# Loads of h tiles by their places, splits moved between engines, rotary tables in two tiles, stores on ScalarE's queue

## The chip, the cores and the metric

The kernel runs on one core of one Trainium2 chip. The metric is device time in microseconds of one execution; for the kernel before it is the median of three runs. The engines are TensorE (PE, matmul and transposes), VectorE (DVE), ScalarE (ACT), GpSimd (POOL) and SyncE (SP), which here only issues DMAs.

## The reference

One layer of an encoder trunk, applied to two groups of 1024 tokens ("prompt" and "sample") with the same weights, in float32:

```python
for each group:                                   # x is (1, 1024, 1024)
    qa, ka, va, qb, kb, vb = split(x @ w_in)      # 2304 columns
    oa = rms_norm(dilated windows, three patterns, joined by their denominators) (rope(qa), rope(ka), va)
    ob = rms_norm(grouped attention(axial_rope(rms_norm(qb)), axial_rope(rms_norm(kb)), vb))
    x = layer_norm(alpha * x + concat(oa, ob) @ w_o)
    x = layer_norm(alpha * x + cross_attention(x, mem))        # 4 heads, 256 memory tokens
    gate, val = split(x @ w_up)                                # 2 x 2816 columns
    h = gelu(depthwise_conv3(gate) + conv_b) * val
    x = layer_norm(alpha * x + h @ w_down)
```

## The kernel before

The two groups run one after the other, each through phase_in (input projection, rotary, stores of q, k, v), attention, phase_mid (output projection, cross attention), ffn_up and ffn_down; between the first group's phase_in and attention stands cross_prep for both. A float32 product is made of three matmuls of rounded operands: every operand is split into a high half (a rounded copy) and a low half (the operand minus the high half), and mm3 (lines 125 to 129) issues high x high, high x low, low x high. So every operand that reaches TensorE costs two instructions elsewhere. split (lines 113 to 115) puts the high half on ScalarE (line 109) and the low half on VectorE (line 115). wsplit (lines 117 to 123) puts both on GpSimd (lines 122 and 123), with act=True the high half on ScalarE and with dve=True the low half on VectorE.

The order of the work on each engine is set by the framework's planner, which runs a simulation of the program in the order in which it is written; it puts an instruction ahead of earlier ones when they are not ready, and each engine then keeps that order. DMAs are issued by SP, in the order of its own list, so that one which waits holds up those behind it.

phase_in: x arrives in eight tiles of 128 tokens through two buffers (xl); x_in (line 295) loads one and splits it, in group 0 tiles 1 and 3 by wsplit and the others by split. Weights come in chunks of 512 columns through three raw buffers (raw, line 82, shared by all phases) and six split tiles (wts). In chunk 0 the first four token tiles are accumulated together, the others follow. The rotary tables (tabs, 128 x 8 x 8 x 64) are one tile; load_tabs (line 310) loads it in group 0 in four DMAs, multiplies half of it by the two norm gains on GpSimd (lines 322 and 327) and stores it to DRAM (tabd), from which group 1 loads it in one DMA (line 312). rope (line 331) multiplies on VectorE (lines 337 and 343) and adds on GpSimd (line 345).

phase_mid and ffn_up: the up projection works on sums and differences of quarters of x and w_up with seven products instead of eight (numbers 1 to 7). x2t (line 900) transposes one tile of normalized x (line 903), evacuates it (lines 908 and 911), and after each second tile forms sums (lines 882 to 888) and splits blocks of them (block, line 867); late (line 894) splits further quarters with pool=True, by wsplit. standardize (line 798) normalizes a tile: statistics on VectorE, a power on GpSimd (line 140), the product on ScalarE (line 807). In ffn_up the first column block, f = 0, is done in two half products: all seven products on the first half of the tokens, with the last x2t after product 5, then all seven on the second half. Its weights are split with the high half on ScalarE and the low half on VectorE for all seven (the dve argument); later blocks use VectorE for 6, 7, 5 and 3.

ffn_down: the 22 tiles of h (128 x 1024) and w_down are multiplied in four passes: tiles 0 to 11 for output columns 0 to 511, tiles 0 to 11 for columns 512 to 1023, tiles 12 to 21 for columns 0 to 511, and the same for the rest. One step takes one h tile against eight token tiles, 24 matmuls of 512 columns. h_in (line 1135) loads an h tile into a raw buffer and splits it into one of 14 slots; tiles 14 to 21 take the slots of tiles 0, 1, 2, 7, 8, 9, 10 and 11. wd_in (line 1144) loads and splits w_down for two steps, through the same raw buffers. In the second pass h_in is called once in each step until all 22 are loaded. In the fourth pass each output tile is normalized by layernorm (lines 780 to 795, with the power at 140) and stored (line 1213).

Of the kernel before, what the change touches and what calls it, by code (L numbers as in the profile page):

```python
# [18 lines left out]
NT = 8  # L19
# [52 lines left out]
class Trunk:  # L72
# [43 lines left out]

    def wsplit(self, hi, lo, raw, act=False, dve=False):
        nc = self.nc
        if act:
            self.copy(hi, raw)  # L120
        else:
            nc.gpsimd.tensor_scalar(hi, raw, 1.0, 0.0, op0=ALU.mult, op1=ALU.add)  # L122
        return (nc.vector if dve else nc.gpsimd).tensor_sub(lo, raw, hi.bitcast(F32))  # L123
# [14 lines left out]
    def rpow(self, out, ms, _=None):  # L138

        self.nc.gpsimd.tensor_tensor(out, ms, self.neghalf[:, :1].to_broadcast(list(ms.shape)), op=ALU.pow)  # L140
# [144 lines left out]
    def phase_in(self, g, S, tabd):  # L285
# [6 lines left out]
        xl, tabp, wk, vs, t1p = P("xl", 2, "left"), P("tabs"), P("rope", 2), P("vs", 3), P("t1p", 4)  # L292
        xT = []

        def x_in(ct):
            xt = xl.tile([128, 8, 128], F32, name="xt")
            t8 = self.t8.tile([128, 2, 8, 128], F32R, name="t8")
            n = 2 if g == 0 and ct == 0 else 1
            for j in range(n):
                k = slice(j * 8 // n, (j + 1) * 8 // n)  # L300
                nc.sync.dma_start(xt[:, k], xd[ct, :, k])
                if g == 0 and ct in (1, 3):
                    self.wsplit(t8[:, 0, k], t8[:, 1, k], xt[:, k])
                else:
                    self.split(t8[:, 0, k], t8[:, 1, k], xt[:, k])
            xT.append(t8)

        tabs = tabp.tile([128, NT, 8, 64], F32, name="tabs")

        def load_tabs():  # L310
            if g:
                nc.sync.dma_start(tabs, tabd)
                return

            with self.tc.issue_after(self.w_dma.ins):
                for j in range(0, NT, 2):
                    nc.sync.dma_start(tabs[:, j:j + 2], a["tabs"][:, j:j + 2])
            for q, gn in ((0, "q_norm_g"), (1, "k_norm_g")):
                gt = tabp.tile([128, 64], F32, name=f"gt{q}")
                nc.sync.dma_start(gt, bcast_rows(a[gn], 64))  # L320
                c, s = tabs[:, :, 4 + 2 * q], tabs[:, :, 5 + 2 * q]
                nc.gpsimd.tensor_mul(c, c, gt[:, None, :].to_broadcast([128, NT, 64]))
                sv = s.rearrange("p t (a b e) -> p t a b e", a=2, b=2)
                gv = gt.rearrange("p (a b e) -> p a b e", a=2, b=2)
                for aa in range(2):
                    for b in range(2):
                        nc.gpsimd.tensor_mul(sv[:, :, aa, b], sv[:, :, aa, b],
                                             gv[:, None, aa, 1 - b].to_broadcast([128, NT, 16]))
            nc.sync.dma_start(tabd, tabs)

        def rope(p, nh, ct, tab, half):
# [4 lines left out]
            c, s = tabs[:, ct, tab], tabs[:, ct, tab + 1]  # L336
# [50 lines left out]
        for ch in range(5):  # L387
            if ch == 1 and g == 0:
                self.conv_constants()
            if ch == 4 and g == 0:  # L390
                self.mem_in(xl)
# [418 lines left out]
    def phase_mid(self, g, S, o2s, ob, G, U, yD):  # L810
# [56 lines left out]
        def block(i, j, src, pool=False):  # L867

            c = slice(j * 128, j * 128 + 128)
            (self.wsplit if pool else self.split)(bt[i][0][:, :, c], bt[i][1][:, :, c], src.rearrange("p (k t) -> p k t", k=4))  # L870
# [162 lines left out]
    def ffn_up(self, B, todo, hD):  # L1033
# [74 lines left out]
        ready = [weights(0, (6, 1, 7, 5, 2, 4, 3))]  # L1108
        for f in range(NFF):
            e = begin(f)  # L1110
            if f == 0:

                for i in ORDER:
                    prod(e, i, 0)
                    if i == 5:
                        x2t()
# [38 lines left out]
    def ffn_down(self, B, yD, hD, out):  # L1155
# [23 lines left out]
        for lo, hi, n in ((0, K0, 0), (0, K0, 1), (K0, NFF, 0)):  # L1179
# [6 lines left out]
            for f in range(lo, hi):  # L1186
# [10 lines left out]
                elif len(hs) < NFF:  # L1197
# [9 lines left out]
        for ct in range(NT):  # L1207
# [5 lines left out]
            nc.sync.dma_start(out[ct * 128:(ct + 1) * 128], yt(ct))  # L1213
# [89 lines left out]
```

## Time and profile before

| | |
|---|---|
| median of the runs | 3304.3 us (3292.97, 3304.3, 3304.65) |
| profiled execution | 3311.24 us, span 3309.4 us |
| granted TensorE clock, mean of the span | 0.981 |
| TensorE matmul | 3190.4 us busy, 96% of the span |
| TensorE weight load | 2712.0 us, 82% |
| VectorE | 1772.7 us, 54% |
| GpSimd | 1559.3 us, 47% |
| ScalarE | 1210.5 us, 37% |

Times within the profile are microseconds from the start of the span. A busy TensorE is not TensorE at its peak, so its idle stretches and its granted clock are read beside its busy time. A wait in the profile has the engine's instruction, and behind an arrow the instruction that it waited for; a window is a stretch of the span with the busy time and the count of instructions of each engine in it. Group 0 fills the first half of the span, group 1 begins at about 1747.

### The profile page before, as it was taken

Reading aid. Unit: us, or ns where it says so; the run is one execution under the profiler, and the core shown is the slowest. Engines: PE = TensorE matmul, PEld = TensorE weight load, DVE = VectorE, ACT = ScalarE, POOL = GpSimd, SP = SyncE. Lnnn points to the kernel's source line nnn. Section 1 sums busy time; section 2 is a strip of 40 time slices with the busy share of each in tenths; the row PEclk is TensorE's granted clock in tenths of the full one; section 3 lists DMA queues with packets and bytes.
Section 4 is the critical chain, followed back from the end, with each engine's and each line's share of the span. In section 5 each row is a group of like instructions: output and inputs, shape, how many; then the busy total and the mean of one; then the engine's idle time right before and its main releaser. Section 6 shows DMA issues by size and latency. Waiting matters only on the chain.

```text
span 3309.4 us, 42941 instructions
## 1 busy us (share of the span) xinstructions
PE 3190.4 (96%) x16425; PEld 2712.0 (82%) x16425; DVE 1772.7 (54%) x2975; ACT 1210.5 (37%) x2355; POOL 1559.3 (47%) x1173
## 2 busy tenths in 40 slices
PE   7999999999999999999898999999999999999988
PEld 6888899888887888888687889888888788888867
DVE  5242156884536766556135255688444676665414
ACT  2122156882333434331002126688143443333101
POOL 4473500774435655543336450277343665554242
PEclk9999999999999999999899999999999999999999
DMA  6455486003121222235225368500211132224421
GB/s 230 129 169 187 167 213 173 14 7 99 42 77 51 78 88 83 89 129 177 92 71 190 118 164 185 142 14 23 90 51 64 58 96 77 83 77 170 141 89 51
DMA packets 292578, 351.63 MB, mean 106 GB/s; under 512 B 17980, under 2 KB 211732, under 8 KB 291476
## 3 DMA queue, kind: packets, MB, share of 16 engines
q1 hardware_dynamic: 292084, 348.82, 34.3%
q8 instruction: 129, 2.11, 0.3%
q14 instruction: 77, 0.63, 0.1%
q10 hardware_dynamic: 288, 0.07, 0.0%
HBM read 252.24 MB, written 100.79 MB: 107 GB/s over the span
## 4 chain that ended last, share of the span: by engine, by line
PE 89%; DMA 3%; DVE 2%; POOL 2%; ACT 1%; issue 1%; SPq 1%; POOLq 0%; ACTq 0%; DVEq 0%
PE pS L1069 11%; PE pT L1069 7%; PE pO L1069 7%; PE pO L127 7%; PE pO L129 7%; PE pO L128 7%; PE pT L127 7%; PE pT L129 7%; PE pT L128 7%; PE pO L697 4%; PE pT L686 3%; PE pS L670 3%; PE pO L593 2%; PE pS L554 2%; PE pS L127 2%; PE pS L128 2%
## 5 line engine op out<-in xcount | busy, mean ns | idle before, releaser
L123 POOL TENSOR_TENSOR wts<-raw,wts 128x512 fp32r<-128x512 f32 (+1 forms) x229 | 470.8, 2062 | 220.0 <-ACT wts L109 215.4
L1069 PE MATMUL pS<-t,wts 128*128 128x512 f32 (+1 forms) x1656 | 378.7, 382 | 1.1 <-DVE t L115 1.0
L1069 PEld LDWEIGHTS pS<-t,wts 128*128 128x128 f32 x1656 | 304.4, 190 | 60.5 <-DVE t L115 1.2
L127 PE MATMUL pT<-wts,t 128*128 128x512 f32 (+1 forms) x864 | 340.0, 394 | 8.7 <-ACT wts L109 8.3
L129 PE MATMUL pT<-wts,t 128*128 128x512 f32 (+1 forms) x864 | 335.9, 389 | 11.2 <-DVE t L115 11.2
L128 PE MATMUL pT<-wts,t 128*128 128x512 f32 (+1 forms) x864 | 336.0, 389 | 0.5 <-DVE wts L123 0.5
L127 PE MATMUL pO<-wts,t 128*128 128x512 f32 (+1 forms) x816 | 322.1, 395 | 5.4 <-DVE t L343 3.8
L128 PE MATMUL pO<-wts,t 128*128 128x512 f32 (+1 forms) x816 | 317.2, 389 | 4.2 <-POOL wts L123 4.2
L129 PE MATMUL pO<-wts,t 128*128 128x512 f32 (+1 forms) x816 | 316.6, 389 | 0.3 <-DVE t L115 0.3
L122 POOL TENSOR_SCALAR wts<-raw 128x1024 fp32r<-128x1024 f32 (+1 forms) x88 | 102.2, 1165 | 380.0 <-DMA raw<-w_down 242.3
L1069 PE MATMUL pT<-t,wts 128*128 128x512 f32 (+1 forms) x1104 | 258.0, 382 | 1.4 <-ACT t L109 1.0
L1069 PE MATMUL pO<-t,wts 128*128 128x512 f32 (+1 forms) x1104 | 256.9, 380 | 0.5 <-ACT res L109 0.4
L122 POOL TENSOR_SCALAR ptb<-praw 128x512 fp32r<-128x512 f32 x116 | 72.8, 628 | 382.0 <-ACT praw L109 230.9
L1069 PEld LDWEIGHTS pT<-t,wts 128*128 128x128 f32 x1104 | 203.2, 190 | 41.2 <-ACT t L109 1.2
L1069 PEld LDWEIGHTS pO<-t,wts 128*128 128x128 f32 x1104 | 202.0, 189 | 40.1 <-ACT res L109 0.5
L129 PEld LDWEIGHTS pT<-wts,t 128*128 128x128 f32 x864 | 163.6, 189 | 44.2 <-DVE t L115 11.7
L127 PEld LDWEIGHTS pT<-wts,t 128*128 128x128 f32 x864 | 164.4, 190 | 40.1 <-ACT wts L109 8.3
L128 PEld LDWEIGHTS pT<-wts,t 128*128 128x128 f32 x864 | 163.9, 190 | 32.7 <-DVE wts L123 1.0
L127 PEld LDWEIGHTS pO<-wts,t 128*128 128x128 f32 x816 | 155.9, 191 | 37.2 <-issue 4.2
L128 PEld LDWEIGHTS pO<-wts,t 128*128 128x128 f32 x816 | 154.8, 190 | 34.3 <-POOL wts L123 4.5
L129 PEld LDWEIGHTS pO<-wts,t 128*128 128x128 f32 x816 | 154.6, 189 | 31.9 <-DVE t L115 0.8
L673 DVE TENSOR_REDUCE mn<-pS 128x1 f32<-128x1024 f32 x128 | 155.9, 1218 | 42.1 <-PE pS L670 41.0
(272 smaller groups left out, 6804.7 us busy)
## 6 DMA issues: line engine op xcount, KB each, us to landing
raw<-w_up SPq DMA_DIRECT2D x88, 512.0 KB, 4.4
hD<-d SPq DMA_DIRECT2D x44, 512.0 KB, 5.2
raw<-hD SPq DMA_DIRECT2D x44, 512.0 KB, 4.5
raw<-w_down SPq DMA_DIRECT2D x44, 512.0 KB, 3.9
raw<-w_in SPq DMA_DIRECT2D x32, 512.0 KB, 4.5
kst<-ka SPq DMA_DIRECT2D x32, 512.0 KB, 10.3
qa<-vs SPq DMA_DIRECT2D x16, 512.0 KB, 3.9
ka<-vs SPq DMA_DIRECT2D x16, 512.0 KB, 3.6
```

The source lines that it names most:

```text
L122: nc.gpsimd.tensor_scalar(hi, raw, 1.0, 0.0, op0=ALU.mult, op1=ALU.add)
L123: return (nc.vector if dve else nc.gpsimd).tensor_sub(lo, raw, hi.bitcast(F32))
L127: mm(out, sh, mh, start=start, stop=False)
L128: mm(out, sh, ml, start=False, stop=False)
L129: mm(out, sl, mh, start=False, stop=stop)
L554: nc.tensor.matmul(o, qq, kk[hl], start=hl == 0, stop=hl == 1)
L593: nc.tensor.matmul(po[:, n * 64:(n + 1) * 64], pt[:, n, j], v, start=j == 0, stop=j == 1)
L670: nc.tensor.matmul(p[:, ns], q[:, ct * 128:(ct + 1) * 128], ks[:, hl, ns], start=hl == 0, stop=hl == 1)
L673: nc.vector.tensor_reduce(mn, p, axis=X, op=ALU.min)
L686: nc.tensor.transpose(p[:, c * 128:(c + 1) * 128], s[:, k * 128:(k + 1) * 128], self.ident)
L697: nc.tensor.matmul(po[:, :256], bd["v"][:, k, h // 4], hl[l][:, k].rearrange("p a b -> p (a b)"), start=k == 0 and l == 0, stop=k == 7 and ...
L1069: nc.tensor.matmul(p, w[:, x, k], b[l][:, k, cs], start=i in (1, 6, 7, 5) and k + x + l == 0, stop=k == 3 and x == 1, skip_group_check=True)
```

## The change

- x_in: in group 0, tiles 4 to 7 are split by the new hsplit (high half on ScalarE, low half on GpSimd) instead of split.
- block with pool=True, called by late, uses hsplit instead of wsplit: the high half goes from GpSimd to ScalarE.
- The rotary tables are two tiles of four token tiles each, in two pools, loaded and stored separately. The multiplication by the gains is a function of its own, called in group 0 before chunk 2 instead of right after the load, in twenty instructions instead of ten.
- ffn_up: for f = 0 the low halves of weights 2, 4 and 3 go to GpSimd, and the last x2t is written after all seven first half products instead of after product 5.
- ffn_down: in the second pass h_in is called in steps 0 to 4 and 8 to 11 only, and h tile 21 is left to the third pass, which loads it at its own step.
- The output stores are issued by ScalarE instead of SP.
- rpow loses an argument that was not used.

```diff
+    def hsplit(self, hi, lo, src):
+        self.wsplit(hi, lo, src, True)
...
-        xl, tabp, wk, vs, t1p = P("xl", 2, "left"), P("tabs"), P("rope", 2), P("vs", 3), P("t1p", 4)
+        xl, tabp, wk, vs, t1p = P("xl", 2, "left"), [P("tab0"), P("tab1")], P("rope", 2), P("vs", 3), P("t1p", 4)
...
                     self.wsplit(t8[:, 0, k], t8[:, 1, k], xt[:, k])
+                elif g == 0 and ct > 3:
+                    self.hsplit(t8[:, 0, k], t8[:, 1, k], xt[:, k])
...
-        tabs = tabp.tile([128, NT, 8, 64], F32, name="tabs")
+        tabs = [tabp[i].tile([128, 4, 8, 64], F32, name="tabs") for i in range(2)]
...
+            for i in range(2):
+                if g:
+                    nc.sync.dma_start(tabs[i], tabd[:, 4 * i:4 * i + 4])
+                    continue
+
+                with self.tc.issue_after(self.w_dma.ins):
+                    for j in range(0, 4, 2):
+                        nc.sync.dma_start(tabs[i][:, j:j + 2], a["tabs"][:, 4 * i + j:4 * i + j + 2])
+
+        def gain_tabs():
             for q, gn in ((0, "q_norm_g"), (1, "k_norm_g")):
...
+            for i in range(2):
+                nc.sync.dma_start(tabd[:, 4 * i:4 * i + 4], tabs[i])
...
+            if ch == 2 and g == 0:
+                gain_tabs()
...
-            (self.wsplit if pool else self.split)(bt[i][0][:, :, c], bt[i][1][:, :, c], src.rearrange("p (k t) -> p k t", k=4))
+            (self.hsplit if pool else self.split)(bt[i][0][:, :, c], bt[i][1][:, :, c], src.rearrange("p (k t) -> p k t", k=4))
...
-        ready = [weights(0, (6, 1, 7, 5, 2, 4, 3))]
+        ready = [weights(0, (6, 1, 7, 5))]
...
                 for i in ORDER:
                     prod(e, i, 0)
-                    if i == 5:
-                        x2t()
+                x2t()
...
-                elif len(hs) < NFF:
+                elif len(hs) < NFF - 1 and len(hs) - 12 <= f - (3 if f > 4 else 0) and not 4 < f < 8:
+
                     self.h_in(hD)
...
-            nc.sync.dma_start(out[ct * 128:(ct + 1) * 128], yt(ct))
+            nc.scalar.dma_start(out[ct * 128:(ct + 1) * 128], yt(ct))
```

## Rows read from the trace of the kernel before

**Rows 1.** TensorE's waits, longest first: instruction, releaser, us in total, times, longest.
```profile
PE pS L127 <- POOL wts L122: 29.8, 4, 7.5
PE pS L903 <- ACT res L807: 11.8, 2, 6.1
```
**Rows 2.** Windows of 50 us: PE, PEld, DVE, ACT, POOL busy (count), clock, DMA, GB/s.
```profile
1500.00:1550.00 50.00, 50.00 (x222) 41.42 (x221) 34.94 (x28) 6.55 (x7) 19.04 (x8) 1.00 0.64 220
1550.00:1600.00 50.00, 45.53 (x201) 37.35 (x199) 8.53 (x9) 4.24 (x4) 7.76 (x4) 0.99 0.24 80
1600.00:1650.00 50.00, 39.59 (x150) 31.83 (x151) 12.63 (x12) 4.24 (x4) 20.17 (x12) 0.81 0.29 97
...
3150.00:3200.00 50.00, 35.10 (x136) 28.17 (x136) 13.39 (x13) 5.30 (x5) 17.82 (x10) 0.86 0.27 90
```
**Rows 3.** Windows at the start of group 0, columns as above.
```profile
28.40:42.00 13.60, 1.41 (x6) 0.75 (x5) 13.59 (x4) 0.28 (x1) 12.39 (x9) 0.64 0.37 154
42.00:46.00 4.00, 4.00 (x10) 3.15 (x11) 0.54 (x2) 0.00 (x0) 1.27 (x1) 0.51 0.71 262
```
**Rows 4.** Second pass of ffn_down in time: start, us, instruction, [idle before, releaser].
```profile
1571.41 2.60 SPq L1138 DMA_DIRECT2D raw<-hD  x2
...
1595.56 1.06 ACT L109 ACTIVATE t<-raw 128x1024 fp32r<-128x1024 f32 x1 [26.14 <-PE pO L129]
...
1597.90 0.38 SPq L1147 DMA_DIRECT2D raw<-w_down  x1
...
1603.01 0.80 PE L127 MATMUL pS<-wts,t 128*128 128x512 f32 x1 [7.48 <-POOL wts L122]
```
**Rows 5.** Instructions on tile xt until 70 us: ns least, median, most; starts.
```profile
L115 DVE TENSOR_TENSOR t<-xt,t x7: 692/1224/12685, 4.5 to 61.6; 128x1024 fp32r<-128x1024 f32 x5, 128x512 fp32r<-128x512 f32 x2
```
**Rows 6.** Start of group 0 in time, GpSimd and TensorE.
```profile
28.38 1.06 POOL L122 TENSOR_SCALAR t<-xt 128x1024 fp32r<-128x1024 f32 x1
...
33.84 2.36 POOL L123 TENSOR_TENSOR t<-xt,t 128x1024 fp32r<-128x1024 f32 x1
...
41.93 0.80 PE L129 MATMUL pT<-wts,t 128*128 128x512 f32 x1 [11.24 <-DVE t L115]
```
**Rows 7.** Instructions on tile tabs until 80 us, GpSimd's: ns least, median, most.
```profile
L327 POOL TENSOR_TENSOR tabs<-tabs,gt x8: 461/467/482, 23.8 to 27.9; 128x128 f32<-128x128 f32 x8
...
L322 POOL TENSOR_TENSOR tabs<-tabs,gt x2: 1293/1293/1293, 22.5 to 25.4; 128x512 f32<-128x512 f32 x2
```
**Rows 8.** A window in which chunks 2 and 3 are projected, columns as above.
```profile
150.00:200.00 50.00, 50.00 (x230) 41.45 (x229) 15.69 (x41) 6.95 (x12) 30.28 (x23) 1.00 0.39 121
```
**Rows 9.** Windows at the start of the up projection, group 0.
```profile
1060.00:1066.00 6.00, 0.42 (x2) 0.42 (x3) 5.45 (x9) 4.28 (x7) 6.00 (x6) 0.76 0.31 88
1066.00:1088.00 22.00, 20.47 (x120) 18.99 (x119) 16.07 (x25) 8.66 (x17) 14.32 (x9) 0.83 0.14 49
```
**Rows 10.** Start of the up projection in time, group 0.
```profile
1053.23 3.48 DVE L123 TENSOR_TENSOR wts<-raw,wts 128x512 fp32r<-128x512 f32 x2
...
1065.58 1.97 PE L903 MATMUL pS<-ident,res 128*128 128x128 f32 x8 [5.79 <-ACT res L807]
...
1070.38 1.50 ACT L911 ACTIVATE res<-pS,ln2c 128x128 f32<-128x128 f32 x4
```
**Rows 11.** From group 0 to group 1 in time.
```profile
1746.13 1.99 ACT L109 ACTIVATE t<-xt 128x1024 fp32r<-128x1024 f32 x2
...
1766.91 0.46 SPq L1213 DMA_DIRECT2D out<-res  x1
...
1767.42 0.42 SPq L312 DMA_DIRECT2D tabs<-tabd  x1
...
1778.78 0.69 DVE L337 TENSOR_TENSOR t<-pO,tabs 128x512 f32<-128x512 f32 x1 [6.46 <-DMA tabs<-tabd]
...
1780.28 0.76 PE L127 MATMUL pO<-wts,t 128*128 128x512 f32 x1 [3.76 <-DVE t L343]
```
**Rows 12.** Window behind the wait for the tables, columns as above.
```profile
1776.00:1785.00 9.00, 5.24 (x18) 3.92 (x17) 6.22 (x13) 2.12 (x2) 2.96 (x3) 0.81 0.55 222
```

More of the change, by code (lines that the diff above doesn't have):

```diff
@@ L136, in dma, with rpow @@
             self.sp_last = self.nc.sync.dma_start(out, in_)
-    def rpow(self, out, ms, _=None):
+    def rpow(self, out, ms):
         self.nc.gpsimd.tensor_tensor(out, ms, self.neghalf[:, :1].to_broadcast(list(ms.shape)), op=ALU.pow)
@@ L306, in x_in @@
             xT.append(t8)
-        tabs = tabp.tile([128, NT, 8, 64], F32, name="tabs")
+        tabs = [tabp[i].tile([128, 4, 8, 64], F32, name="tabs") for i in range(2)]
         def load_tabs():
[L311 to L317, printed above, removed]
+            for i in range(2):
[6 more added lines that the diff above has]
+        def gain_tabs():
             for q, gn in ((0, "q_norm_g"), (1, "k_norm_g")):
-                gt = tabp.tile([128, 64], F32, name=f"gt{q}")
+                gt = tabp[1].tile([128, 64], F32, name=f"gt{q}")
                 nc.sync.dma_start(gt, bcast_rows(a[gn], 64))
-                c, s = tabs[:, :, 4 + 2 * q], tabs[:, :, 5 + 2 * q]
-                nc.gpsimd.tensor_mul(c, c, gt[:, None, :].to_broadcast([128, NT, 64]))
-                sv = s.rearrange("p t (a b e) -> p t a b e", a=2, b=2)
                 gv = gt.rearrange("p (a b e) -> p a b e", a=2, b=2)
[L325 to L329, printed above, removed]
+                for t in tabs:
+                    c, s = t[:, :, 4 + 2 * q], t[:, :, 5 + 2 * q]
+                    nc.gpsimd.tensor_mul(c, c, gt[:, None, :].to_broadcast([128, 4, 64]))
+                    sv = s.rearrange("p t (a b e) -> p t a b e", a=2, b=2)
+                    for aa in range(2):
+                        for b in range(2):
+                            nc.gpsimd.tensor_mul(sv[:, :, aa, b], sv[:, :, aa, b],
+                                                 gv[:, None, aa, 1 - b].to_broadcast([128, 4, 16]))
+            for i in range(2):
+                nc.sync.dma_start(tabd[:, 4 * i:4 * i + 4], tabs[i])
         def rope(p, nh, ct, tab, half):
@@ L335, in rope @@
             t2 = wk.tile([128, 512], F32, name="t2")[:, :nh * 64]
-            c, s = tabs[:, ct, tab], tabs[:, ct, tab + 1]
+            c, s = [tabs[ct // 4][:, ct % 4, i] for i in (tab, tab + 1)]
             nc.vector.tensor_mul(t1.rearrange("p (h e) -> p h e", h=nh), p.rearrange("p (h e) -> p h e", h=nh),
```

## The prediction

> **What bounds the kernel now.** The page gives the first answer: TensorE is busy nearly all the span, so only its holes and the stretches in which its clock is halved can be won. I therefore read the waits of TensorE first, longest total on top [rows 1]: four waits of 7.5 us for GpSimd's weight splits in the down projection, and two of about 6 us for ScalarE's standardizing at the start of the up projection. The second view cuts the span into stretches of 50 us and counts matmuls. A full stretch of 512-column matmuls has 222, that is 50 / 222 = 0.2252 us each; 1550 to 1600 has 201, 1600 to 1650 has 150, and in the second group 3150 to 3200 has 136 [rows 2]. Counting what is missing takes in both the wait and the slow matmuls that follow it, so I price every hole in missing matmuls. The same count shows the start: 28.4 to 42 has 6 matmuls where 60.4 fit, 42 to 46 has 10 where 17.8 fit, at a granted clock of 0.51, which is the lower of the two levels, 1.2 GHz [rows 3]. That is (54.4 + 7.8) x 0.2252 = 14.0 us. The third view, the order of time around each hole, gives the causes below.
>
> **Loads of h.** In the second pass of ffn_down, h tiles 17, 18 and 19 are loaded as soon as a raw buffer is free (1571.41), but their slots are still read by TensorE, so all three raw buffers sit full. The split of h17 runs at 1595.56, after 26.14 us of ScalarE idleness ended by TensorE; only then does a raw buffer come free, the w_down load goes out at 1597.90, and TensorE starts again at 1603.01 after 7.48 us [rows 4]. Two steps later the same happens with h18 and h19. Price in missing matmuls: group 0 (21 + 72) x 0.2252 = 20.9 us, group 1 86 x 0.2252 = 19.4 us [rows 2], together 40.3. The change calls h_in at steps 0 to 4, not at 5 to 7, then one each at 8 to 11, each in the step in which the old reader of its slot has just ended, and leaves h21 to the third pass. In that order the buffers that h17 to h19 hold come after the load of weight tile 4 and of tile 5; behind them stands tile 6, first needed in the third pass. It waits for h18's split at the end of step 8, plus a chain as in rows 4 from split to matmul, 7.45 us (1595.56 to 1603.01). Three steps of 24 matmuls lie between, 72 x 0.2252 = 16.2 us, so some 8.8 us of cover are left; if that cover went, the price would be the old one, about 10 us for each late tile (40.3 / 4). I take the whole 40.3, with 38 (a rest of 0.6 us for each late tile) and 41 as bounds.
>
> **Start of group 0.** VectorE's low half of x4 took 12.685 us where the median of that form is 1.224 [rows 5]; GpSimd was busy 12.39 of the 13.60 us around it [rows 3], and TensorE waited 11.24 us for the result [rows 6]. So VectorE stood still while GpSimd worked through its list. The change gives the low halves of x4 to x7 to GpSimd. On GpSimd such a half takes 2.36 us [rows 6], 1.14 us more than VectorE's median. The Trainium skill, GPSIMD Engine Reference, section Engine selection, advises VectorE for two-input arithmetic because GpSimd is about twice as slow; the trace agrees in size, and by that alone four halves would cost 4.6 us and the gain would be 9.4. The Trainium skill, SBUF — State Buffer, section Who interferes with whom, says that whichever of the two engines issues first holds the shared port for that instruction; by it VectorE would have waited for one GpSimd instruction, 2.36 us, and not 11; here the row decides, and it shows a wait through the whole list. The best end: x3's two halves (1.06 and 2.36 from 28.38) and then x4's run at once, done at 34.2; TensorE has x3's 24 matmuls, 5.4 us, from 29.4 to 34.8, so nothing but the first microsecond is lost and the gain is 13. The worst end: GpSimd keeps its old order and x4's low half comes last, at 28.38 + 12.39 + 2.36 = 43.1; TensorE can do x3's matmuls meanwhile but little else, loses 43.1 − 28.4 − 5.4 = 9.3 us and some slow matmuls, and the gain is 3. The gain multiplications of the tables also leave this place: two of 1.293 and eight of 0.467 us, 6.3 us [rows 7], which stood right ahead of 28.38 and pressed all later work into one list. As twenty instructions on half tables they cost 6.3 (by element) to 12.6 us (by instruction), and GpSimd has 50 − 30.28 = 19.7 us free in 150 to 200 with no matmul missing [rows 8], so I cost them at nothing; were that room gone, it would be up to 12.6 us. Their two table stores pass behind them on SP's queue. With them gone I take a value nearer to the best end, 10.
>
> **Start of the up projection, twice.** From 1060 to 1066 TensorE does 0.42 us of work while GpSimd is busy 6.00 of 6.00 and VectorE 5.45; the 22 us after it hold 20.47 us of matmul at a granted clock of 0.83 [rows 9]. At two levels that is 34% of the time at the lower one, half of which is lost: 22 x 0.17 = 3.7. With 5.6 and 1.5 of idle time the place costs 10.8 us a group. TensorE waits 5.79 us for the last tile's standardizing; two VectorE low halves of weights, 3.48 us together from 1053.23, lie ahead of that tile's sum [rows 10]. The change moves the low halves of weights 2, 4 and 3 to GpSimd, takes six high halves of the late blocks from GpSimd to ScalarE (busy 4.28 of 6.00 [rows 9]) and lets the last three half products, 36 matmuls of 256 columns, go ahead of the transposes. At half of 0.2252 each these fill 4.1 us of the 5.79. What is late next is the way back: transposes, evacuation, sums, splits, second half products. It used to hide behind the same 36 matmuls, and its evacuation began at 1070.38, 2.8 us after the transposes ended (1065.58 + 1.97) [rows 10]; it can now begin at once. So moving the work alone gives the 2.8 us, and the shorter list on VectorE up to 3.5 more, less what GpSimd, full already, gives back. Bounds per group: 0 (the wait only changes place) and 9 (2.8, 3.5 and most of the 3.7 of slow matmuls); I take 5, twice 10.
>
> **Group change.** The tables are loaded in one piece at 1767.42, right behind the last output store at 1766.91; VectorE's first rotary product waits 6.46 us for them until 1778.78, and TensorE 3.76 us behind that, until 1780.28 [rows 11]. 1776 to 1785 has 18 matmuls where 40 fit, 22 x 0.2252 = 5.0 us [rows 12]. Half of the tables now has a pool of its own, and the first four row tiles need only that. I take 4.5, bounds 2 and 5. Sixteen stores move from SP's queue to ScalarE's, each an issue of 0.46 us [rows 11] on an engine with room; behind a waiting store there stand, on ScalarE, the next tile's normalizing and the high halves of group 1's x tiles, for which TensorE waits. In the last pass TensorE does not wait for normalizing, so this is nothing, save in the rival below.
>
> **Sum.** 10 + 40.3 + 10 + 4.5 = 64.8 us. The profiled execution took 3311.2 us, 6.9 more than the median of the runs: 3311.2 − 64.8 = 3246.4 for such an execution, and 3239.5, so 3240, for the median.
>
> **Rivals.** (a) Only the h loads and part of the rest pay: GpSimd's list stays at the start (3) and at the up projection the wait changes place (0), with 38 and 2: 43 us, 3261. For it speaks that GpSimd is full in both places [rows 3, 9] and gets more low halves. (b) The h loads don't do what they say: the held buffers delay the first two weight tiles of the third pass instead, four waits of 10 us moved and not removed; 24.5 us remain, 3280. The 8.8 us of cover speak against it. (c) Slower: the buffers stay held right through the third pass, so that every one of its five weight tiles comes late in both groups, 10 x 10 us, while the 40.3 and the other 24.5 come in: 35 us more, 3339. It decides from the seventh late tile on. Against it: after h20 no h tile but h21 takes a raw buffer in that pass. (d) A store waits on ScalarE ahead of group 1's first x tiles: their high halves would slip from 1746.13 to the last store's 1766.91 [rows 11], 20.8 us at once: 3261. Against it: the planner would have to place a store that is ready later ahead of work that is ready.
>
> **How the numbers follow.** Forecast 0.62, (a) 0.22, (b) 0.05, (c) 0.03, (d) 0.05, and 0.03 for nothing measurable because the planner's new order loses elsewhere what is won. The forecast's own bounds, best ends 13 + 41 + 18 + 5 = 77 us, reach 3227, and the spread of the three runs (11.3 us below the median at most) some microseconds further: 3218. The upper end takes in (a) and (d): 3264. What can be told from no change is 0.5%, 16.5 us: faster 0.94, same 0.03, slower 0.03.
>
> **What would show it.** Right: in the waits of TensorE the line for GpSimd's weight splits in ffn_down is gone, and the two stretches in the second pass count 222; in the first 60 us VectorE has no low half over 2 us and TensorE no wait over 4; the transposes at the up start follow the third product with a wait under 2 us, and the evacuation follows them at once; the rotary product of group 1 waits for no table. Wrong: waits of 7 us at the third pass, a ScalarE queue standing before a store while x tiles are due, or a GpSimd list over 10 us long ahead of x4's low half.

## The result and the profile after

| | kernel before | changed kernel |
|---|---|---|
| median, first comparison | 3301.5 us (4 executions, 3292.97 to 3304.65) | 3264.07 us (4, 3259.23 to 3265.19) |
| ratio, 95% interval | | 0.9888 (0.9865 to 0.991) |
| median, second comparison on another chip | 3294.22 us (7, 3292.49 to 3301.18) | 3263.28 us (4, 3261.21 to 3269.8) |
| ratio, 95% interval | | 0.9909 (0.9893 to 0.9926) |
| profiled execution | 3311.24 us, span 3309.4 | 3265.19 us, span 3263.4 |

So the change makes the kernel about 1% faster: 37 us by the first comparison, 31 by the second. The forecast was 3240, and the measured 3264.07 lies just past the upper end of its range. Of the 28 executions of the kernel before that were timed in this study, 21 took 3289 to 3299 us and 7 took 3301 to 3311, and the profiled one that the prediction rests on is the longest of all.

TensorE's waits in the changed kernel, as in [rows 1] (instruction, releaser, us in total, times, longest):

```profile
PE pT L699 <- DVE pta L591: 10.5, 2, 5.8
PE pS L1082 <- DVE res L1091: 8.7, 2, 4.8
...
PE pT L1082 <- DVE wts L126: 4.7, 4, 1.3
PE pO L131 <- POOL wts L126: 4.2, 1, 4.2
...
PE pS L916 <- ACT res L820: 0.8, 1, 0.8
```

The two lines of [rows 1] have gone: no GpSimd split of ffn_down (29.8 us) is left, the one wait on POOL's L126 belongs to the group change, and the standardizing holds TensorE for 0.8 us and not 11.8. But a wait that was not there before now stands second, behind one in attention (10.5 us in all): 4.8 us in group 0 and 3.9 in group 1, at line 1082 (a product of the up projection) on line 1091 (a sum over a product in PSUM, where the products land). The windows, as in [rows 2, 3 and 9]:

```profile
28.40:42.00 13.60, 10.38 (x48) 7.95 (x47) 4.24 (x9) 2.14 (x3) 13.60 (x8) 1.00 0.77 264
42.00:46.00 4.00, 4.00 (x21) 3.34 (x20) 1.59 (x4) 1.66 (x2) 4.00 (x3) 1.00 0.90 267
1060.00:1066.00 6.00, 6.00 (x44) 6.00 (x44) 1.49 (x5) 2.14 (x6) 0.00 (x0) 0.81 0.23 90
1066.00:1088.00 22.00, 18.64 (x104) 16.18 (x103) 18.68 (x23) 8.73 (x17) 15.03 (x10) 0.84 0.17 48
...
1550.00:1600.00 50.00, 50.00 (x222) 41.39 (x221) 6.78 (x5) 5.31 (x5) 14.69 (x8) 1.00 0.31 106
1600.00:1650.00 50.00, 50.00 (x223) 41.38 (x222) 11.16 (x11) 3.18 (x3) 35.86 (x20) 1.00 0.42 137
...
3150.00:3200.00 50.00, 50.00 (x223) 41.39 (x222) 6.66 (x8) 1.06 (x1) 23.32 (x14) 1.00 0.21 64
```

The second pass of ffn_down is full: 222 and 223 matmuls where 201, 150 and 136 stood. The start has 48 matmuls in 28.4 to 42 where 6 stood. At the up projection the 22 us from 1066 hold 104 matmuls at a clock of 0.84, against 120 at 0.83; but the stage begins at 1044.30 here and at 1053.01 in the first profile of the kernel before, so that these two windows do not hold the same work. The next table compares by instruction.

Both traces have 16,425 TensorE instructions, so one can subtract the start of the n-th in one from that of the n-th in the other, and see at which n the difference grows. This gives the table below: us won against the first profile of the kernel before, stretch by stretch. "Start" ends at instruction 600; the up projection is counted from 5550 to 5950 and 13,300 to 13,700, the second pass from 7950 to 8100 and 15,700 to 16,050, the group change from 8550 to 9000; "rest" is everything else, mostly attention, and moves by some us from execution to execution. The last column is the up stage by itself, from the start of its first matmul to that of its last, in each group; in the first profile of before it is 435.4 and 434.4.

| kernel | start | up, group 0 | 2nd pass, 0 | group change | up, group 1 | 2nd pass, 1 | rest | sum | up stage |
|---|---|---|---|---|---|---|---|---|---|
| predicted | 10 | 5 | 20.9 | 4.5 | 5 | 19.4 | 0 | 64.8 | |
| changed kernel | 10.8 | −5.1 | 20.8 | 4.6 | −4.8 | 19.7 | 0.1 | 46.0 | 440.5, 439.3 |
| the same, second profile | 10.5 | −6.2 | 20.8 | 4.2 | −4.9 | 19.7 | 2.0 | 45.9 | 441.6, 439.4 |
| before, second profile | 12.3 | 0.2 | 0.1 | 0.2 | 0.2 | 0.2 | 4.8 | 18.0 | 435.1, 434.2 |
| h_only | 12.4 | −0.2 | 20.8 | −0.2 | −2.4 | 19.7 | 1.1 | 51.2 | 435.5, 436.8 |
| u_all | 10.2 | −0.4 | 20.8 | 5.6 | −0.2 | 19.7 | −5.9 | 49.8 | 435.8, 434.6 |
| u_all_b | 9.7 | 0.3 | 20.8 | 6.0 | 0.3 | 19.7 | −4.5 | 52.2 | 435.1, 434.2 |
| u_wts | 10.5 | −7.2 | 20.8 | 4.3 | −7.2 | 19.7 | 2.4 | 43.3 | 442.6, 441.7 |
| u_x2t | 10.3 | −4.6 | 20.8 | 5.1 | −4.8 | 19.7 | 1.7 | 48.2 | 439.9, 439.3 |
| u_block | 10.1 | −0.1 | 20.8 | 5.6 | −0.7 | 19.7 | −3.8 | 51.6 | 435.5, 435.2 |
| e_l3 | 10.3 | −5.2 | 20.8 | −1.0 | −5.3 | 19.7 | 2.2 | 41.5 | 440.6, 439.8 |
| e_ydo | 11.4 | −0.7 | 20.8 | 5.0 | −0.6 | 19.7 | −0.7 | 54.9 | 436.1, 435.1 |
| e_npb | 11.5 | −0.3 | 20.8 | 4.7 | −1.6 | 19.7 | 2.1 | 56.9 | 435.7, 436.1 |
| u_x | 2.3 | −5.8 | 20.8 | 4.5 | −4.5 | 19.7 | 0.3 | 37.1 | 441.2, 439.0 |
| u_gain | 8.9 | −4.6 | 20.8 | 5.2 | −6.0 | 19.7 | 0.9 | 44.8 | 439.9, 440.4 |
| u_store | 11.0 | −4.8 | 20.8 | 4.5 | −4.5 | 19.7 | 3.3 | 50.0 | 440.1, 438.9 |
| u_all_start | 1.8 | 0.3 | 20.8 | 4.8 | −2.4 | 19.7 | −5.2 | 39.7 | 435.1, 436.8 |

Three terms came out to the microsecond, and one has the wrong sign: the up projection lost 5 us in each group where 5 were to be won. Each run below has one profile. How far two profiles of one kernel differ can be read from the table: the stages of before, of the changed kernel and of u_all (u_all_b is its second profile) come out within 1.1 us of each other in either group. So 4 to 5 us in both groups are clear of that. The experiments look for the cause of the loss first, and then test the start.

### The profile page after: what moved, and what is told of

It reads as the page before. It is cut to its first block, busy times and chain, and to the rows that moved or that the text cites. A ratio compares the mean times of both kernels' runs of the same rounds, so it can differ in the third digit from the quotient of the medians.

```text
span 3263.4 us, 42968 instructions
## 1 busy us (share of the span) xinstructions
PE 3177.4 (97%) x16425; PEld 2701.0 (83%) x16425; DVE 1765.6 (54%) x2965; ACT 1220.5 (37%) x2373; POOL 1560.4 (48%) x1175
## 4 chain that ended last, share of the span: by engine, by line
PE 89%; DMA 4%; DVE 3%; POOL 1%; ACT 1%; SPq 1%; issue 1%; ACTq 0%; POOLq 0%; DVEq 0%
PE pS L1082 11%; PE pT L1082 7%; PE pO L1082 7%; PE pO L130 7%; PE pO L132 7%; PE pO L131 7%; PE pT L132 7%; PE pT L130 7%; PE pT L131 7%; PE pO L710 4%; PE pT L699 3%; PE pS L683 3%; PE pO L606 2%; PE pS L567 2%; PE pS L132 2%; PE pS L131 2%
## 5 line engine op out<-in xcount | busy, mean ns | idle before, releaser
L126 POOL TENSOR_TENSOR wts<-raw,wts 128x512 fp32r<-128x512 f32 (+1 forms) x233 | 475.6, 2047 | 233.7 <-ACT wts L109 228.7
```

## The start of the up projection: one edit loses ten microseconds

The changed kernel there, group 0, in time; to be read against [rows 10]:

```profile
1044.44 3.46 DVE L126 TENSOR_TENSOR wts<-s,wts 128x512 fp32r<-128x512 f32 x2
1045.60 3.44 POOL L126 TENSOR_TENSOR wts<-raw,wts 128x512 fp32r<-128x512 f32 x2
...
1049.91 0.32 SPq L1002 DMA_DIRECT2D yD<-res  x1
...
1053.38 1.50 ACT L924 ACTIVATE res<-pS,ln2c 128x128 f32<-128x128 f32 x4 [2.97 <-DMA yD<-res]
...
1056.85 0.39 ACT L109 ACTIVATE res<-pS 128x256 f32<-128x256 f32 x1
...
1058.90 2.93 PE L1082 MATMUL pS<-t,wts 128*128 128x256 f32 x12 [4.76 <-DVE res L1091]
...
1063.38 1.03 PE L916 MATMUL pS<-ident,res 128*128 128x128 f32 x8
...
1069.03 0.48 PE L1082 MATMUL pT<-t,wts 128*128 128x256 f32 x1 [1.74 <-ACT t L109]
```

The last transposes (1063.38) now follow a product with no wait, as forecast. But the evacuation of the transposes before them, which writes into the tile that the store of normalized x (yD, issued at 1049.91) still reads, waits 2.97 us for that store to land. ScalarE works in order, so the high halves of weights and blocks and the copy of product 1 (1056.85) stand behind it; VectorE's sum needs that copy, and the bank that it reads is what TensorE waits for, 4.76 us. Behind the transposes only two products, 24 matmuls, are left for the way back (evacuation, sums, splits) to hide under, and TensorE waits for it (1.74). Which edit did it?

**u_all, all three edits undone.**

```diff
-            (self.hsplit if pool else self.split)(bt[i][0][:, :, c], ...
+            (self.wsplit if pool else self.split)(bt[i][0][:, :, c], ...
...
-        ready = [weights(0, (6, 1, 7, 5))]
+        ready = [weights(0, (6, 1, 7, 5, 2, 4, 3))]
...
                     prod(e, i, 0)
+                    if i == 5:
+                        x2t()
-                x2t()
```

> The changed kernel with its three edits at the start of the up projection undone: late blocks split by wsplit, low halves of weights 2, 4 and 3 of the first column block on VectorE, the last x2t after product 5. The up projection runs from its first to its last matmul 435.4 us before and 440.5 after in group 0, 434.4 and 439.3 in group 1. Theory: these three edits, and nothing else of the change, make the up projection longer, so both stages fall back to 435 and 434.5 and the whole kernel is 10 us shorter than the changed one, about 3254. Rival: the stage got longer because the work ahead of it ends earlier (another phase of the DMAs and of the lists), then it stays at 439 to 441 and the kernel at 3264.

Measured: stage 435.8 and 434.6, as before the change; median 3256.39 us (3252.97 to 3261.69), ratio to before 0.9872 (0.9851 to 0.9893). The wait for the standardizing is back in its old size:

```profile
PE pS L916 <- ACT res L820: 11.5, 2, 5.8
```

So the three edits together remove a wait of 5.8 us in each group and make the stage 5 us longer. Next, one undone at a time.

**u_wts, u_x2t and u_block.** The same diff, of which u_wts has only the line of the weights, u_x2t only the place of the last transposes, and u_block only the blocks' high halves.

> The changed kernel with one edit undone: the low halves of weights 2, 4 and 3 of the first column block go back to VectorE. Theory A (these three low halves on GpSimd collide with VectorE's low halves for weights 7 and 5, whose pair took 3.46 us instead of 1.79, and delay the standardizing behind them): the up projection falls by at least 3 us per group, to 437 or less in group 0. Theory B (the place of the last x2t) and theory C (high halves of the late blocks in ScalarE's list): it stays within 1 us of 440.5.

> The changed kernel with one edit undone: the last x2t is written after product 5 again. Theory B (with the transposes behind more products the way back, that is evacuation, sums and splits, is exposed): the up projection falls by at least 3 us per group. Theories A and C: it stays within 1 us of 440.5, or gets longer by up to 4 as the wait for the standardizing comes back ahead of the last three half products.

> The changed kernel with one edit undone: the late blocks are split by GpSimd alone again. Theory C (ScalarE's list holds the copy of product 1 behind the late blocks' high halves, and TensorE waits 4.8 us for the sum made from it): that wait falls under 2 us and the up projection by at least 3 us per group. Theories A and B: the stage stays within 1 us of 440.5 or gets longer by up to 3, since GpSimd has six more instructions.

Measured: u_wts 442.6 and 441.7, 1 to 2.4 us worse than the two profiles of the changed kernel, against theory A; u_x2t 439.9 and 439.3, no change, against theory B (written after product 5 or after all seven, the last transposes come to stand in the same place, at 1064.02 and 1063.38); u_block 435.5 and 435.2, theory C. So the high halves of the late blocks on ScalarE are the loss. With them back on GpSimd the other two edits win nothing over the kernel before (435.4 and 434.4): the old wait returns, longer. The end of VectorE's part in the kernel before, and then u_block:

```profile
1058.31 0.15 DVE L804 TENSOR_SCALAR brs<-bmv 128x1 f32<-128x1 f32 x1
```

```profile
1048.78 0.15 DVE L817 TENSOR_SCALAR brs<-bmv 128x1 f32<-128x1 f32 x1
...
1057.62 0.55 POOL L143 TENSOR_TENSOR brs<-brs,neghalf 128x1 f32<-128x1 f32 x1
...
1059.27 1.23 ACT L820 ACTIVATE res<-res,brs 128x1024 f32<-128x1024 f32 x1
...
1060.55 1.97 PE L916 MATMUL pS<-ident,res 128*128 128x128 f32 x8 [6.88 <-ACT res L820]
```

VectorE's part is done 1.9 us after the stage's first matmul (1046.88), where it took 5.3 in the kernel before (1058.31 less 1053.01): 3.4 us earlier, as the prediction had it (up to 3.5). But the power on GpSimd then stands 8.8 us in that engine's list, behind splits of which the edits have added some. The way was cleared on one engine and blocked on the next. The evacuation waits for its store here too, 2.98 us, but with four products, 48 matmuls, behind the transposes to hide it:

```profile
1064.03 1.51 ACT L924 ACTIVATE res<-pS,ln2c 128x128 f32<-128x128 f32 x4 [2.98 <-DMA yD<-res]
```

**e_l3, the high halves on ScalarE for the last quarter's three blocks alone.**

```diff
-            (self.hsplit if pool else self.split)(bt[i][0][:, :, c], ...
+            (self.hsplit if i == 3 else self.wsplit if pool else self.split)(bt[i][0][:, :, c], ...
```

> The changed kernel with the high halves of the blocks on ScalarE for the third quarter alone (the three blocks written last), and back on GpSimd for the other six. The changed kernel loses about 3 us a group ahead of the last transposes, where the low halves of six blocks collide with VectorE's weights, and about 5 behind them, less 2.3 won at the wait for the standardizing. Theory F: the six earlier blocks cost the first part and the last three the second: stage 437 to 439. Rival 1: the last three alone cost all: 440 or more. Rival 2: the six alone cost all: 434.5 to 436.

Measured: 440.6 and 439.8, rival 1: these three blocks alone cost all of it. But not by the way of the changed kernel, since no wait for a store stands here:

```profile
1053.09 0.38 ACT L109 ACTIVATE res<-pS 128x256 f32<-128x256 f32 x1 [3.08 <-POOL t L126]
...
1053.99 2.93 PE L1082 MATMUL pS<-t,wts 128*128 128x256 f32 x12 [3.94 <-DVE res L1091]
...
1062.47 1.03 PE L916 MATMUL pS<-ident,res 128*128 128x128 f32 x8
...
1067.94 0.58 PE L1082 MATMUL pT<-t,wts 128*128 128x256 f32 x1 [4.43 <-ACT t L109]
```

The copy of product 1 waits for the low halves of these blocks on GpSimd, and the transposes come behind the last of the seven products, so that all of the way back is bare (4.43). What the two slow orders share is two waits, one for the bank of product 1 (4.76 and 3.94 us) and one for the way back (1.74 and 4.43, against 0.99 in the kernel before), in place of the one at the transposes, behind which products were left to hide the way back.

This run also lost the gain of the group change (−1.0 against 4.6). The first thing that meets the eye there is a store that stands in ScalarE's list until GpSimd has finished its tile, and a high half of x behind it, ahead of which ScalarE is idle for 6.58 us. But the changed kernel has the same wait, 6.91 us, and wins 4.6 us there, so this does not explain the loss. First e_l3, then the changed kernel:

```profile
1741.57 0.37 ACTq L1226 DMA_DIRECT2D out<-res  x1
1741.99 1.06 ACT L109 ACTIVATE t<-xt 128x1024 fp32r<-128x1024 f32 x1 [6.58 <-POOL res L805]
...
1753.11 1.23 DVE L115 TENSOR_TENSOR t<-xt,t 128x1024 fp32r<-128x1024 f32 x1 [5.84 <-ACT t L109]
1754.25 0.68 DVE L348 TENSOR_TENSOR t<-pO,tabs 128x512 f32<-128x512 f32 x1
...
1755.74 0.47 PE L130 MATMUL pO<-wts,t 128*128 128x512 f32 x1 [3.43 <-ACT t L109]
```

```profile
1742.94 2.09 ACT L109 ACTIVATE t<-xt 128x1024 fp32r<-128x1024 f32 x2 [6.91 <-POOL res L805]
...
1748.31 0.69 DVE L348 TENSOR_TENSOR t<-pO,tabs 128x512 f32<-128x512 f32 x1
```

What differs is VectorE's list. In e_l3 the first rotary product (1754.25) stands behind a low half of x that waits 5.84 us for its high half; in the changed kernel it runs at 1748.31, ahead of that low half, and TensorE goes on without a wait. In every other version of the changed kernel the rotary product also comes first, and these win 4.2 to 6.0 us. So rival (d), the store ahead of the x tiles, did occur in small, in the changed kernel as in e_l3, but TensorE did not feel it; that VectorE's order is what e_l3 pays for is read from the two traces and was not tested by a run.

**e_ydo, no wait for the store.**

```diff
-                nc.sync.dma_start(yD[ct], yt(ct))
+                nc.sync.dma_start(yD[ct], yt(min(ct, 5)))
```

> The changed kernel, with the stores of the last two tiles of normalized x (tiles 6 and 7) storing tile 5 instead, so that the evacuation of the transposes, which writes into the stored tile, waits for no store; part of the stored data is therefore another tile's. Theory D: in the changed kernel the evacuation on ScalarE waits 2.97 us for the store of tile 6 to land, the copy of product 1 stands behind it in ScalarE's list, and TensorE waits 4.76 us for that: without the store's wait the evacuation begins within 1 us of the transposes' end, TensorE's wait falls to about 2, the up stage by 2 to 4 us in each group (436 to 438). Rival: the length of ScalarE's and GpSimd's lists sets it, and the stage stays at 439 to 441.

Measured: 436.1 and 435.1, that is 4.4 and 4.2 us less, theory D:

```profile
1050.14 1.50 ACT L924 ACTIVATE res<-pS,ln2c 128x128 f32<-128x128 f32 x4 [0.72 <-PE pS L916]
...
1054.83 1.69 PE L1082 MATMUL pS<-t,wts 128*128 128x256 f32 x12 [1.68 <-DVE res L1091]
```

The evacuation starts 1.2 us after its transposes begin and not 3.4, and TensorE's wait falls from 4.76 to 1.68. ScalarE, VectorE and GpSimd have the same instructions in the same order there as in the changed kernel. So in that order the wait for the store is the loss, 4.4 and 4.2 of 5 us. All waits of TensorE in the first 45 us of the stage add up to 7.2 us in the kernel before, 10.3 in the changed kernel, 11.0 in e_l3 and 7.2 in e_ydo: 3.1 of the 5 us stand in these waits, and the rest is not divided further.

**e_npb, u_block with the power of the last tile left out.**

```diff
-        self.rpow(rs[:, 0:1], rs[:, 0:1])
+        if not last:
+            self.rpow(rs[:, 0:1], rs[:, 0:1])
...
-                self.standardize(yt(ct), st[ct])
+                self.standardize(yt(ct), st[ct], ct > 6)
```

> The kernel with the blocks' high halves back on GpSimd (the run in which the wait for the standardizing came back, 6.88 us), with the power of the standardizing of the last tile left out. Theory E: the wait is the power standing in GpSimd's list, 8.8 us behind its operands (1048.78 to 1057.62); without it the standardizing starts at about 1050 and the wait at the last transposes falls under 2 us, the up stage by 3 to 6 us in each group (430 to 432.5). Rival: VectorE's or ScalarE's list holds the standardizing as long, or the way back takes the time: stage 434 to 436.

Measured: the first half of theory E holds, the second falls. The wait at the transposes drops from 6.88 to 1.91 us, but the stage stays at 435.7 and 436.1, because the copy of product 1 is late again and TensorE waits 5.34 us for its bank:

```profile
1050.36 1.17 PE L917 MATMUL pS<-ident,res 128*128 128x128 f32 x8 [1.91 <-DVE res L922]
...
1056.87 2.93 PE L1083 MATMUL pS<-t,wts 128*128 128x256 f32 x12 [5.34 <-DVE res L1092]
```

Five versions of this place (before, u_all, u_block, e_ydo and e_npb) end within 434 to 437 us, whichever wait is removed. What would take the stage below that no run shows.

## The loads of h alone

**h_only**, the kernel before with one line:

```diff
-                elif len(hs) < NFF:
+                elif len(hs) < NFF - 1 and len(hs) - 12 <= f - (3 if f > 4 else 0) and not 4 < f < 8:
```

> The kernel before with the rule for the loads of h alone. Theory of the prediction: the holes at the two late weight tiles of the second pass of ffn_down close in both groups and nothing else moves. By the comparison of the two traces, matmul by matmul, these two stretches gave 20.8 and 19.7 us, so the span falls by 40 (38 to 42) from 3309.4 to about 3269, the windows 1550 to 1600 and 1600 to 1650 hold 222 matmuls, and all other stretches stay within 1.5 us, save attention (3). Rival: part of the 40 came from other edits (stores or tables off SP's queue, which then pass the w_down loads earlier): under 34.

Measured: 20.8 and 19.7 us in the two stretches, none of it from other edits. Median 3260.79 us (3257.5 to 3266.13) against 3294.34, ratio 0.9896 (0.9865 to 0.9926). One line gives what the whole change gives. But the span fell by 51.2 and not 40: the hole at the start, 12.4 us, was gone too, in a kernel whose instructions up to ffn_down are those of the kernel before. The up projection of group 1 came out 2.4 us longer, outside the 1.5 that were expected: its source is the same, but the planner put some of its instructions in another order.

## The start of group 0: a hole that comes and goes

**before_b**, the kernel before once more, with no edit:

> The kernel before once more, unchanged, for a second profiled execution. The run with the loads of h alone had no hole at the start (its low half of x3 took 2.09 us), although its first 50 us are the same instructions in the same order as before. Theory 1: the standstill of VectorE (12.69 us) is an accident of single executions, one in four or so, as the times of before lie at 3290 to 3298 us in most executions and at 3304 to 3311 in the others: this profile has a span of 3288 to 3297 and most likely no low half over 4 us in the first 60 us, and then TensorE's instructions up to the 600th come 10 to 13 us earlier than in the first profile. Theory 2: the hole belongs to the kernel before, and something in the other run removed it: span 3300 to 3310, the low half again over 10 us.

Measured: span 3291.4, theory 1. VectorE's low halves of x in the first 70 us, second profile of before, to be read against [rows 5]:

```profile
L115 DVE TENSOR_TENSOR t<-xt,t x7: 693/1227/1865, 4.4 to 49.2; 128x1024 fp32r<-128x1024 f32 x5, 128x512 fp32r<-128x512 f32 x2
```

The longest takes 1.87 us, not 12.69 (the one that stood is that of x4; the expectation calls it x3), and 28.4 to 42 has 54 matmuls, more than the 48 of the changed kernel. So the hole of [rows 3, 5, 6] is no property of the kernel's order but of single executions. That the 7 of 28 executions at 3301 us and above are those that have it is likely by size (12 us) but only shown for the profiled one at 3311, as its absence is for the one at 3293.

**u_x and u_gain**, the two edits at the start undone one by one in the changed kernel:

```diff
-                elif g == 0 and ct > 3:                                  # u_x
-                    self.hsplit(t8[:, 0, k], t8[:, 1, k], xt[:, k])
...
                 load_tabs()
+                if g == 0:                                               # u_gain
+                    gain_tabs()
...
-            if ch == 2 and g == 0:
-                gain_tabs()
```

> The changed kernel with the low halves of x4 to x7 back on VectorE; the multiplications by the gains stay before chunk 2. Theory 1: VectorE stands still while GpSimd works through its list, and the change pays because these low halves leave VectorE: back on it the hole at 30 to 42 us comes back, start 6 to 11 us later than in the changed kernel, a VectorE low half of over 6 us. Theory 2: the list was long only because the multiplications by the gains (6.3 us) stood in it; with them gone it is short, the start is 0 to 4 us later than in the changed kernel and no low half takes over 6 us.

> The changed kernel with the multiplications by the gains right after the tables' load again; the low halves of x4 to x7 stay on GpSimd. Theory 1 (the moved low halves are what pays, the multiplications cost little): start 0 to 3 us later than in the changed kernel. Theory 2 (the list is what counts): the low halves of x4 to x7 stand behind 6 to 12 us of multiplications on GpSimd itself, and the start is 5 to 11 us later.

Measured: u_x starts 8.5 us later than the changed kernel (2.3 against 10.8), and the hole is there:

```profile
L115 DVE TENSOR_TENSOR t<-xt,t x7: 692/1219/10947, 4.5 to 56.5; 128x1024 fp32r<-128x1024 f32 x5, 128x512 fp32r<-128x512 f32 x2
```

u_gain starts 1.9 us later. Both times are what theory 1 said, but neither run tested the multiplications, because these never left their place: whether they are written before chunk 2 or right after the load, the planner puts all twenty ahead of x3's high half. The four larger ones in the changed kernel, in u_gain and in u_x, and then that high half in the changed kernel and in u_gain:

```profile
L333 POOL TENSOR_TENSOR tabs<-tabs,gt x4: 737/737/741, 19.0 to 24.5; 128x256 f32<-128x256 f32 x4
L333 POOL TENSOR_TENSOR tabs<-tabs,gt x4: 734/737/742, 19.1 to 24.6; 128x256 f32<-128x256 f32 x4
L331 POOL TENSOR_TENSOR tabs<-tabs,gt x4: 734/737/739, 18.6 to 24.1; 128x256 f32<-128x256 f32 x4
...
26.29 1.07 POOL L125 TENSOR_SCALAR t<-xt 128x1024 fp32r<-128x1024 f32 x1
26.42 1.05 POOL L125 TENSOR_SCALAR t<-xt 128x1024 fp32r<-128x1024 f32 x1
```

In the first 120 instructions of GpSimd and 150 of VectorE, u_gain has the order of the changed kernel. So its 1.9 us are no price of the multiplications; the other eleven profiles with the low halves on GpSimd win 9.7 to 11.5 us at the start, u_gain 8.9. What is left of the two edits in the traces is the move of the low halves, and u_x undoes that. What the start would be with the multiplications out of this place no run shows.

**after_b, u_all_b and u_all_start**, side by side on one chip: the changed kernel and u_all again, and u_all with both edits of the start undone as well (in the trace only the low halves have moved: the multiplications run from 19.5 to 26.8).

> The changed kernel once more, unchanged, beside the next two on one chip. By the profiles it keeps the 40 us of the second pass and the 4.5 of the group change and pays 10 at the up projection: median 3260 to 3265.

> The changed kernel without its three edits at the start of the up projection, beside the two others. By the profiles it is 9 to 10 us faster than the changed kernel: median 3251 to 3256. Rival: the 10 us of single profiles are lost elsewhere in most executions, and the two medians lie within 3 us.

> The kernel of the run before this one, and the start of group 0 put back as well (low halves of x4 to x7 on VectorE, multiplications by the gains right behind the tables' load). If the hole comes only in one execution of four, the median is within 3 us of the run before this one, and single executions lie 10 to 13 us above the others, while the run before has none such. If the hole comes in most executions, the median is 8 to 12 us longer.

| kernel | median us (lowest to highest) | ratio to before, 95% interval |
|---|---|---|
| after_b | 3263.28 (3261.21 to 3269.8) | 0.9909 (0.9893 to 0.9926) |
| u_all_b | 3256.33 (3255.36 to 3259.25) | 0.9887 (0.9872 to 0.9902) |
| u_all_start | 3264.32 (3261.84 to 3271.54) | 0.9913 (0.9899 to 0.9928) |

The edits at the up projection cost 7.0 us of the median, less than the 9 to 10 of the stages. The spans of the profiles differ by 3.7 (u_all) and 6.3 (u_all_b): in u_all, u_all_b, u_block and u_all_start the rest, attention, loses 3.8 to 5.9 us, in the other versions of the changed kernel it lies between −0.7 and 3.3. Whether that belongs to those four kernels is open. u_all_start is 8.0 us slower than u_all_b, so the low halves on GpSimd are worth 8.0 us there; this is neither of the two cases written down but near the second: its profile has the hole (11.46 us for one low half), and its fastest execution is slower than the slowest of u_all_b. In this order, with the tables split, the hole seems to come in most executions, in that of the kernel before in few. Of the five profiles with these low halves on VectorE three have the hole (before, u_x, u_all_start: 12.69, 10.95, 11.46 us) and two don't (1.72 in before_b, 2.09 in h_only); of the twelve with them on GpSimd none has. What decides between the two is open: in the first profile of before VectorE issued 0.25 us ahead of the end of a GpSimd instruction and stood still, in the second profile 0.65 ahead of one, and got in at the next.

## The output stores

**u_store**, the stores back on SP's queue:

```diff
-            nc.scalar.dma_start(out[ct * 128:(ct + 1) * 128], yt(ct))
+            nc.sync.dma_start(out[ct * 128:(ct + 1) * 128], yt(ct))
```

> The changed kernel with the output stores back on SP's queue. Theory of the prediction: the stores' queue pays nothing, the two tables tiles do: every stretch within 1 us of the changed kernel, the group change still 4 to 5.5 us shorter than before. Rival: the tables' load still stands behind the last store on SP, so the first rotary product waits again, and 2 to 5 us of the group change are lost.

Measured: the group change wins 4.5 us as with the stores on ScalarE (4.6); every other stretch is within 0.4 us of the changed kernel but for the rest (3.3). The queue of the stores pays nothing. That the two tiles of tables do is left by elimination, since h_only, without them, wins nothing there (−0.2), and every other edit of this place was undone in some run; the tables alone were not. u_all remains the fastest version that was timed: 7.0 us faster than the changed kernel on the same chip.

## Why the prediction was wrong, point by point

- **Loads of h: right.** 40.3 us were forecast and 40.5 came. Counting missing matmuls priced the hole of each group to within 0.3 us; the 8.8 us of cover at the third pass held, since TensorE has no wait at all in ffn_down.
- **Start of the up projection: the step that failed.** Taken at +5 a group, it was −5, and outside the bounds of 0 and 9. The mistake was to let 0 ("the wait only changes place") be the worst case of work that moves between three busy engines. The rows did say that GpSimd was busy 6.00 of 6.00 us [rows 9], and the prediction named that ScalarE would take six high halves, but costed them at nothing by its 4.28 of 6.00. It did not follow what stands in ScalarE's order there: an evacuation that waits for a store, and behind it the copy that frees a PSUM bank; that is 4.4 us a group (e_ydo). And it priced the way back behind the transposes at nothing, where TensorE waits 1.74 us (0.99 before); two and not three half products went ahead of them, wherever they were written (u_x2t).
- **Start of group 0: right in size against that one profile, wrong as a term of the median.** 10 us were forecast and 10.8 came by the two traces. But most executions of the kernel before, by their times 21 of 28, have no such hole, and against its second profile (12.3) the changed kernel starts 1.5 us later. Part of the mechanism was wrong as well: the multiplications by the gains were to leave this place and did not (19.0 to 26.3 in the changed kernel). The move of the low halves gave 8.5 us of it, and 2.3 are left without that move (u_x), where the multiplications begin at 18.6 and not at 22.5. The Trainium skill, SBUF — State Buffer, section Who interferes with whom, has the one that issues second blocked for the whole of the other's instruction; two of the five profiles fit that (a wait of under 1 us and then the work), while in three VectorE stood through a whole row of GpSimd instructions, eight of them in the first profile of before (28.38 to 40.80 us).
- **Group change: right,** 4.5 against 4.6, and not by the queue of the stores. Against rival (d) the prediction said that the planner would not put a store that is ready later ahead of work on the x tiles; it did so (ScalarE idle for 6.91 us), but TensorE did not wait for it.
- **From the profile to the median: wrong by 5.8 us.** 6.9 us were taken off because the profiled execution stood that far above the median of three. The changed kernel's profiled execution stands 1.1 above its own. Between the two profiles of before lie 18.0 us, 12.3 of them the hole and 4.8 the rest, mostly attention; whether the hole was part of the 6.9 us is not shown, since two of the three executions of that median lie above 3301 us themselves. The account closes: 64.8 + 6.9 were forecast and 46.0 + 1.1 came, 24.6 us apart; 20 of it is the up projection (+10 to −10) and 5.8 the offset, less 1.2 by the other terms.

Of the rivals, (a) and (d) both gave 3261 and came nearest. (a) did so by other terms: its start and its group change were too small and its zero at the up projection too good. (d) had the store's wait, but not its cost.

## What to carry to other kernels

Before work is moved to an engine with free time, read what stands in that engine's order at that place: an instruction there that waits for a DMA holds up everything that is put behind it, however low the busy share. A hole that one profile shows should be looked for in a second one before it is priced, above all when the profiled execution is longer than the median. Where three engines pass work to one another, removing the named wait says little of the gain; a loss belongs in the range. And where a planner sets the order, an edit in the source is no proof that an instruction moved: the trace is, as with the multiplications here.

## What the runs showed of the hardware

A VectorE instruction with two operands in memory can stand still through a row of GpSimd instructions: 10.95 to 12.69 us in three profiles, while the same instruction in the same place took 1.72 and 2.09 in two others. When both engines split weights side by side, each slows the other: two low halves of 128x512 on VectorE took 3.46 us beside GpSimd's two of 3.44 (from 1044.44), against 1.79 for two on VectorE (from 1049.81) and 2.51 for two on GpSimd (from 1066.87) in the kernel before. A store of 128x1024 kept its tile for some 3.5 us from its issue (1049.91 to 1053.38), which is as long as two such low halves side by side; in u_wts it was 5.2 (1050.57 to 1055.80).
